# Adding each expert's output on chip to rows that are read back, instead of letting the DMA add them in DRAM

## The chip, the cores and the metric

The kernel runs on one core of one Trainium2 chip. The metric is the device time of one execution in microseconds (us); a kernel's time is the median of its runs. The engines of the core are TensorE (PE; its weight loads are listed as PEld), VectorE (DVE), ScalarE (ACT), GpSimd (POOL) and SyncE (SP). All of them run their own instruction streams in order and meet through semaphores. Data moves between DRAM and the on-chip memory through 16 DMA engines, which are fed by queues: here one hardware queue (q1) that SP fills, and one software queue (q0) that GpSimd fills.

## The reference

One decoder layer with 512 tokens of width 2048, in fp32: a mixer (sparse attention beside a convolution), cross-attention into 256 memory rows, and a mixture of experts (MoE). The change lies almost wholly in the last part. A token picks the best of 4 groups, and in that group the best two of 8 experts; each expert is a SwiGLU of hidden width 512, and the two outputs are added with their weights:

```python
grp = argmax(xf @ rg_w + rg_b)                    # 1 of 4 groups
top_v, top_i = lax.top_k(le_g, 2)                 # 2 of the group's 8 experts
w_tok = w_grp[:, None] * softmax(top_v)
h = silu(xb @ w_gate[e]) * (xb @ w_up[e])         # the rows of expert e
y = (h @ w_down[e]) * wb[:, None]
out = zeros(...).at[tok_buf].add(y)
x = layer_norm(DEEPNORM_ALPHA * x + out, ln3_g, ln3_b)
```

So each token's row before the last normalisation is the sum of its own row `x2` and of two experts' rows (the kernel divides the weights by alpha instead of scaling `x2`, which the normalisation allows). The order of the two additions doesn't matter beyond rounding.

## The kernel before

Everything up to the MoE is one long PE-bound stretch of 1500 us, in which weights pass through a ring of tiles (`wr`, split on ACT and DVE into two fp32r parts, `wh` and `wl`, L78). In it `bias_setup` (L250ff) makes the table of relative positions: `vec`, written to `vec_d`, and 16 copies to `toe_d`, all issued by SP between loads of `w_in`.

At the end of cross-attention four tiles of 128 tokens are normalised (`rs` on POOL at L150, the scaling on DVE at L161) and transposed for the router (`x2T`, L72). With gain and bias applied (L829, L830, on DVE and POOL), each tile of 1 MB is written twice by SP: to `x2_d` (L831; `x_d` in the profile), from which experts read their rows, and to `acc_d` (L833), onto which the outputs are added. The router then finds for each token its two experts and its place in their lists.

`build` (L1017) turns these into lists, one for each expert, of up to two blocks of 64 tokens. Per expert it makes 8 one-hot matrices `oh` of 128x128 on DVE (L1024) and 8 matmuls (L1025), each with a one-hot matrix as stationary operand and the 4 columns of `rhs` (token number twice, and the weight in two parts) as moving operand. `lists` (L1034) makes from it row numbers `ix` and weights `wl`. Each half of a token row (1024 floats, 4 KB) has its own number; a place that is not filled gets a number out of bounds, for which the transfer does nothing. Two experts are built before the loop, two at its start, and then four at a time, every fourth turn.

The loop over 32 experts (L1142) streams 12 tiles of 1 MB of weights an expert (4 gate, 4 up, 4 down). SP issues each load (`load_next`, L1107) as soon as one of 19 slots `mr` is released, with a row of loads in flight. In turn e, PE does gate and up of expert e (L1275) in four quarters, then transposes the rows of expert e+1 (`prep`, L1263), then the down product of expert e-1 (L1303) and the transposes of the hidden rows (L1291). Work of a second block, which only 4 experts have, stands in `If` blocks of its own (L1152, L1168, L1172, L1175, L1183), which all engines enter or skip on a count. The down product lands in PSUM (`dn`); `scaled` (L1305ff) multiplies it by the weight, one half on ACT and one on DVE (L1309), into `y`; `put_rows` (L1204) writes `y` to the rows of `acc_d` with an indirect DMA that adds to what is there. `gather` (L1209) reads the rows of expert e+2 with an indirect DMA (L1201) into `xe`, of which there are two for each block. Both are issued by POOL on the software queue.

What sets the order: the code is written in program order, a list scheduler orders each engine's stream by priorities, and the engines run it in that order. After the last expert SP reads `acc_d` back and the last normalisation follows.

## Time and profile before

| | us |
|---|---|
| median of 3 runs (2614.37 to 2618.21) | 2615.86 |
| the profiled execution | 2621.89 |
| its span in the profile | 2619.9 |
| PE busy in the span | 2393.8 |
| DVE busy | 1136.1 |
| ACT busy | 727.6 |
| POOL busy | 193.1 |
| start of the first expert's gate and up products | 1551.4 |
| last output of an expert scaled | 2576.8 |

The page divides the span into 40 slices; PE is busy for 90% or more in nearly all of them, and the 16 DMA engines are above 90% only from the MoE on. The table is thus no answer to what bounds the kernel: each stage is read for itself. The profile's times below are microseconds from the start of the span.

### The profile page before, as it was taken

The page shows a single profiled execution, that of the slowest core. Times are in us where ns is not written, and L with a number is a line of the kernel's source. Part 1 is how long each engine was busy: PE and PEld are TensorE (multiplying, and loading weights), DVE is VectorE, ACT ScalarE, POOL GpSimd, SP SyncE. Part 2 cuts the span into 40 slices and gives each one's busy share as a digit, 9 for nine tenths or more (in the row PEclk, how much of TensorE's full clock was granted, in tenths as well). Part 3 has the DMA queues.
Part 4 walks back from the last instruction along what each step waited for, and adds up shares of the span by engine and source line. Part 5 has one row for each costly group of instructions (what it writes and reads, how often), then busy time and mean ns, then how long its engine had stood idle before and what let it go on. Part 6 is the DMA issues. An engine that isn't in the chain of part 4 may idle for free. (4 is left out here: it accounts for less than half of the span.)

```text
span 2619.9 us, 31427 instructions
## 1 busy us (share of the span) xinstructions
PE 2393.8 (91%) x11298; PEld 1566.2 (60%) x11299; DVE 1136.1 (43%) x2406; ACT 727.6 (28%) x1286; POOL 193.1 (7%) x247
## 2 busy tenths in 40 slices
PE   6999899999999999999999968999998889999973
PEld 5788676789878778788888843333333344333320
DVE  5848985488877643543453542111110101101004
ACT  4323125467766522333321310101000001010103
POOL 1100000000000000000000220101000100110101
PEclk9999999989999999999999968999999999999996
DMA  4235324433334533332542397999999999999995
GB/s 139 87 109 172 111 75 118 125 101 121 105 112 132 202 126 105 128 106 96 196 146 97 126 377 303 418 416 412 409 407 408 413 399 416 347 400 415 416 415 220
DMA packets 195539, 617.30 MB, mean 236 GB/s; under 512 B 43241, under 2 KB 92577, under 8 KB 142096
## 3 DMA queue, kind: packets, MB, share of 16 engines
q1 hardware_dynamic: 178048, 568.08, 57.0%
q0 software_dynamic: 17296, 46.66, 5.8%
q8 instruction: 117, 1.92, 0.3%
q14 instruction: 78, 0.64, 0.1%
HBM read 593.64 MB, written 47.23 MB: 245 GB/s over the span
## 5 line engine op out<-in xcount | busy, mean ns | idle before, releaser
L1275 PE MATMUL gu<-mr,xeT 128*64 128x512 f32 x2048 | 539.7, 613 | 56.4 <-DMA mr<-moe_w_up 23.6
L78 DVE TENSOR_TENSOR wl<-wr,wh 128x1024 fp32r<-128x1024 f32 (+1 forms) x248 | 294.5, 1190 | 374.7 <-ACT wh L78 374.0
L78 ACT ACTIVATE wh<-wr 128x1024 fp32r<-128x1024 f32 (+2 forms) x250 | 256.0, 1026 | 618.2 <-PE pd L83 287.6
L1275 PEld LDWEIGHTS gu<-mr,xeT 128*64 128x64 f32 x2048 | 172.1, 139 | 357.5 <-issue 276.9
L1303 PE MATMUL dn<-mr,hT 128*64 128x512 f32 x1152 | 295.4, 603 | 15.3 <-PEq L1183 12.9
L1284 DVE TENSOR_TENSOR h<-gu,sg 64x256 f32<-64x256 f32 x72 | 30.7, 427 | 446.7 <-ACT sg L1283 446.3
L82 PE MATMUL pd<-xT,wh 128*128 128x512 f32 x512 | 203.8, 405 | 15.5 <-DVE v L550 5.3
L83 PE MATMUL pd<-xT,wh 128*128 128x512 f32 x512 | 205.1, 401 | 0.0
L1303 PEld LDWEIGHTS dn<-mr,hT 128*64 128x64 f32 x1152 | 92.3, 138 | 171.6 <-issue 150.5
L84 PE MATMUL pd<-xT,wl 128*128 128x512 f32 x512 | 183.2, 399 | 1.6 <-DVE wl L78 1.6
L1283 ACT ACTIVATE sg<-gu 64x256 f32<-64x256 f32 x72 | 27.0, 375 | 543.2 <-PE gu L1275 526.3
L445 DVE SCALAR_TENSOR_TENSOR acc<-u,wc,acc 128x512 f32<-128x512 f32 x240 | 164.9, 750 | 0.3
L82 PEld LDWEIGHTS pd<-xT,wh 128*128 128x128 f32 x512 | 99.1, 194 | 41.1 <-issue 14.6
L1309 DVE TENSOR_SCALAR y<-dn,wlm 128x512 f32<-128x512 f32 x36 | 27.0, 751 | 220.1 <-PE dn L1303 210.9
L84 PEld LDWEIGHTS pd<-xT,wl 128*128 128x128 f32 x512 | 98.0, 191 | 24.5 <-DVE wl L78 2.3
L83 PEld LDWEIGHTS pd<-xT,wh 128*128 128x128 f32 x512 | 98.7, 193 | 20.7 <-issue 1.2
L1205 POOL DMA_INDIRECT acc_d<-y,ixm x36 | 57.0, 1583 | 729.2 <-ACT xeT L68 257.8
L83 PE MATMUL pd<-x1T,wh 128*128 128x512 f32 x256 | 101.9, 399 | 0.0
L83 PE MATMUL pd<-wl,oT 128*128 128x512 f32 x256 | 100.1, 391 | 1.1 <-DVE wl L78 1.1
L84 PE MATMUL pd<-x1T,wl 128*128 128x512 f32 x256 | 100.5, 398 | 0.0
L84 PE MATMUL pd<-wh,oT 128*128 128x512 f32 x256 | 99.3, 390 | 0.0
L82 PE MATMUL pd<-x1T,wh 128*128 128x512 f32 x256 | 98.5, 400 | 0.8 <-ACT x1T L175 0.8
(410 smaller groups left out, 3940.7 us busy)
## 6 DMA issues: line engine op xcount, KB each, us to landing
mr<-moe_w_down SPq DMA_DIRECT2D x128, 1024.0 KB, 15.7
mr<-moe_w_gate SPq DMA_DIRECT2D x127, 1024.0 KB, 15.9
mr<-moe_w_up SPq DMA_DIRECT2D x127, 1024.0 KB, 16.0
wr<-xa_wkv SPq DMA_DIRECT2D x64, 512.0 KB, 3.7
wr<-w_in SPq DMA_DIRECT2D x112, 256.0 KB, 3.0
wr<-w_out SPq DMA_DIRECT2D x32, 512.0 KB, 3.5
wr<-xa_wq SPq DMA_DIRECT2D x32, 512.0 KB, 3.5
wr<-xa_wo SPq DMA_DIRECT2D x32, 512.0 KB, 3.5
```

The lines of the kernel that those rows point to most:

```text
L78: return self.nc.scalar.activation(h, src, AF.Copy), eng.tensor_tensor(l, src, h.bitcast(F32), op=ALU.subtract)
L82: mm(out, lhsT=ah, rhs=bh, start=start, stop=False)
L83: mm(out, lhsT=ah, rhs=bl, start=False, stop=False)
L84: mm(out, lhsT=al, rhs=bh, start=False, stop=stop)
L445: nc.vector.scalar_tensor_tensor(a, u[:, k:k + S], wc[:, j, k:k + 1], a, op0=ALU.mult, op1=ALU.add)
L1205: self.nc.gpsimd.indirect_dma_start(out=self.acc_d.rearrange("s (h d) -> (s h) d", h=2), out_offset=bass.IndirectOffsetOnAxis(ap=ix, axis= ...
L1275: self.nc.tensor.matmul(bank[64 * a:64 * a + 64], lhsT=xT[:, 4 * q + c, :], rhs=w[a][:, c * 512:(c + 1) * 512], start=(q == c == 0), stop= ...
L1283: nc.scalar.activation(sg[64:128, sl], bank[0:64, sl], AF.Silu)
L1284: nc.vector.tensor_tensor(h[64 * b:64 * b + 64], bank[64:128, sl], sg[64:128, sl], op=ALU.mult)
L1303: self.nc.tensor.matmul(out[j][64 * a:64 * a + 64], lhsT=hT[:, r, :], rhs=w[:, 1024 * a + 512 * j:1024 * a + 512 * j + 512], start=(r == 0 ...
L1309: self.nc.vector.tensor_scalar(y[:, 512:], out[1], wl, None, op0=ALU.mult)
```

## The change

The sum is made on chip. A token's row has two experts; `x2` stays in `xe` after the first one's product, and the output is added to it there. For the second expert, what the first wrote is read back from `acc_d` over `xe`, and the output is added to that.

- `x2` is written to `x2_d` alone. `acc_d` is instead filled with zeros much earlier, in `bias_setup`: a tile of 256 zeros a partition, and four writes of 1 MB in pieces of 1 KB, on SP.
- `xe` has four tiles for the first block and three for the second, seven in place of four; all are cleared on POOL at the start of the MoE.
- `put_rows` and `scaled` become `add_rows`: two DVE operations that read `dn` from PSUM and `xe`, and write `xe`; then an indirect write of `xe`, without the add in the DMA.
- `get_rows(self.acc_d, ...)` reads the rows back, through the list `got`, which holds only tokens whose second expert (in order of number) this is. The column `fo` of `rhs`, made by three operations on POOL, says which it is.
- `build` compares two token tiles at once (two comparisons an expert, 128x256) with one `oh` buffer, takes the 4 columns as stationary operand and the one-hot matrix as moving operand (4 matmuls), and turns the result with two small transposes an expert. It is called for two experts every second turn.
- Two more `If` blocks stand in a turn: the read-back of a second block, and the gather of a second block (which moves from `gather` to after the put).
- If an expert has more than 128 tokens, `acc_d` is first set to `x2` and every row is read back.

```diff
@@ bias_setup
             nc.sync.dma_start(self.vec_d, vec)
+            z = bs.tile([P, 256], F32, name="zero")
+            nc.gpsimd.memset(z, 0.0)
+            for i in range(4):
+                nc.sync.dma_start(self.acc_d[i * P:(i + 1) * P, :].rearrange("p (c d) -> p c d", d=256), z[:, None, :].to_broadcast([P, 8, 256]))
@@ end of cross-attention
-                    nc.sync.dma_start(self.x2_d[i * P:(i + 1) * P, :], x)
-                    self.x2w[i] = nc.sync.dma_start(self.acc_d[i * P:(i + 1) * P, :], x)
+                    self.x2w[i] = nc.sync.dma_start(self.x2_d[i * P:(i + 1) * P, :], x)
@@ router
+        gp = nc.gpsimd.tensor_tensor
+        tt(r1, r1, r2, op=ALU.is_gt)
+        gp(fo, o1, o2, op=ALU.subtract)
+        gp(fo, fo, bc(r1, 32), op=ALU.mult)
+        gp(rhs[:, :, :, 1], fo, o2, op=ALU.add)
-        nc.vector.tensor_copy(rhs[:, :, :, 1], bc(self.tok, 32))
@@ build
         for j in range(n):
-            for b in range(2):
-                for i in range(4):
-                    oh = pool.tile([P, P], F32R, tag="oh", bufs=4, name="oh")
-                    nc.vector.tensor_scalar(oh, self.ios[:, b, :], self.pos[:, i, e0 + j:e0 + j + 1], None, op0=ALU.is_equal)
-                    nc.tensor.matmul(spv[:, 2 * j + b, :], lhsT=oh, rhs=self.rhs[:, i, e0 + j, :], start=(i == 0), stop=(i == 3))
+            for i in range(4):
+                if i % 2 == 0:
+                    oh = pool.tile([P, 2, P], F32R, tag="oh", bufs=1, name="oh")
+                    nc.vector.tensor_tensor(oh, self.ios[:, None, :].to_broadcast([P, 2, P]), self.pos[:, i:i + 2, e0 + j:e0 + j + 1].to_broadcast([P, 2, P]), op=ALU.is_equal)
+                nc.tensor.matmul(sp[:4, j * P:(j + 1) * P], lhsT=self.rhs[:, i, e0 + j, :], rhs=oh[:, i % 2, :], start=(i == 0), stop=(i == 3))
+        for j in range(n):
+            ls = pool.tile([4, 2, 2, 64], F32, tag="ls", bufs=1, name="ls")
+            nc.vector.tensor_copy(ls, sp[:4, j * P:(j + 1) * P].rearrange("p (b o t) -> p b o t", b=2, o=1).to_broadcast([4, 2, 2, 64]))
+            for b in range(2):
+                nc.tensor.transpose(sp[:, m:m + 4], ls[:, b].rearrange("p o t -> p (o t)"), self.ident[:4, :4])
@@ the MoE's tiles
-        self.xe = [[self.mx.tile([P, D // 2], F32, name=f"xe{j}{b}") for b in range(2)] for j in range(2)]
+        self.xes = [[self.mx.tile([P, D // 2], F32, name=f"xe{j}{b}") for j in range(4 - b)] for b in range(2)]
@@ the loop
-                    if (e + 3) % 4 == 0 and e + 3 < NE:
-                        build(e + 3, 4)
+                    if (e + 3) % 2 == 0 and e + 3 < NE:
+                        build(e + 3, 2)
...
-                    self.put_rows(self.scaled(y, self.where[e - 1, 0][1]), self.where[e - 1, 0][0])
+                    self.add_rows(self.xe(e - 1, 0), y, *self.where[e - 1, 0][1::-1])
...
+                if 0 < e < NE:
+                    self.get_rows(self.acc_d, self.xe(e, 0), self.where[e, 0][2])
+                    with tc.If(self.many(e, [T.Pool]) > 64):
+                        self.get_rows(self.acc_d, self.xe(e, 1), self.where[e, 1][2])
+                if e + 2 < NE:
+                    self.gather(e + 2, 1)
@@ the put
+    def add_rows(self, t, out, wl, ix):
+        for a in range(2):
+            x = t[:, 512 * a:512 * a + 512]
+            self.nc.vector.scalar_tensor_tensor(x, out[a], wl, x, op0=ALU.mult, op1=ALU.add)
         self.nc.gpsimd.indirect_dma_start(out=..., in_=t, in_offset=None,
-                                          bounds_check=2 * S - 1, oob_is_err=False, compute_op=ALU.add)
+                                          bounds_check=2 * S - 1, oob_is_err=False)
```

The change also moves instructions. On SP, in `bias_setup`, the loads of `w_in` and the table's writes stood so before the change (`wr` are the ring's weight tiles):

```order
L92 DMA wr_1887<-w_in 128x2x256 x2
L92 DMA wr_1918<-w_in 128x2x256 x2
L92 DMA wr_1949<-w_in 128x2x256 x2
L92 DMA wr_2056<-w_in 128x2x256 x2
L92 DMA wr_2087<-w_in 128x2x256 x2
L268 DMA vec_d_2377<-vec_2387 16x640
```

and on the same queue SP now has:

```order
L92 DMA wr_1887<-w_in 128x2x256 x2
L273 DMA acc_d_83<-zero_2422 1024x1x256
L92 DMA wr_1918<-w_in 128x2x256 x2
L273 DMA acc_d_83<-zero_2422 1024x1x256 x3
L92 DMA wr_1949<-w_in 128x2x256 x2
L92 DMA wr_2056<-w_in 128x2x256 x2
L92 DMA wr_2087<-w_in 128x2x256 x2
L268 DMA vec_d_2377<-vec_2387 16x640
```

One of the four zero writes now stands ahead of the load of tile 1918, and the other three ahead of that of tile 1949.

On DVE, where the last token tile goes through its normalisation (`rs` and L161) to the router's copy `x2T`, with gain and bias (L829, L830) of the tile between, the rows stood so before:

```order
L151 SCALAR_TENSOR_TENSOR rs_12381<-mv_12379,rs_12381 128x1
L161 TENSOR_SCALAR xr1_11116<-xr1_11116,rs_12381 128x512 x2
L829 TENSOR_TENSOR xr1_11116<-xr1_11116,gb2_12125 128x512 x2
L830 TENSOR_TENSOR xr1_11116<-xr1_11116,gb2_12125 128x512
L829 TENSOR_TENSOR xr1_11116<-xr1_11116,gb2_12125 128x512
L830 TENSOR_TENSOR xr1_11116<-xr1_11116,gb2_12125 128x512
L72 COPY x2T_12124<-ptr_12389 128x512
```

and now (lines are 5 further down, L824 having become L829):

```order
L834 TENSOR_TENSOR xr1_11122<-xr1_11122,gb2_12131 128x512 x2
L835 TENSOR_TENSOR xr1_11122<-xr1_11122,gb2_12131 128x512
L834 TENSOR_TENSOR xr1_11122<-xr1_11122,gb2_12131 128x512
L151 SCALAR_TENSOR_TENSOR rs_12384<-mv_12382,rs_12384 128x1
L835 TENSOR_TENSOR xr1_11122<-xr1_11122,gb2_12131 128x512
L161 TENSOR_SCALAR xr1_11122<-xr1_11122,rs_12384 128x512 x2
L829 TENSOR_TENSOR L_11693<-lgp_11127,rbias_11691 128x36
L72 COPY x2T_12130<-ptr_12392 128x512
```

Gain and bias that stood between the normalisation and the copy are now ahead of the normalisation.

On PE, in the turn in which the lists of later experts are made (`oh` one-hot matrices, `tp` their PSUM, `xe` the next expert's rows), before:

```order
L1025 MATMUL tp<-rhs,oh 128x4 x4
L1303 MATMUL dn<-mr,hT 64x512 x5
L1263 MATMUL tp<-ident,xe_12468 128x128 x4
L1025 MATMUL tp<-rhs,oh 128x4 x4
L1275 MATMUL gu<-mr,xeT 64x512 x8
L1025 MATMUL tp<-rhs,oh 128x4 x4
L1263 MATMUL tp<-ident,xe_12468 128x128 x4
L1025 MATMUL tp<-rhs,oh 128x4 x5
```

and now:

```order
L1037 MATMUL tp<-oh,rhs 4x128 x2
L1348 MATMUL dn<-mr,hT 64x512 x3
L1308 MATMUL tp<-ident,xe_12472 128x128 x4
L1037 MATMUL tp<-oh,rhs 4x128 x2
L1320 MATMUL gu<-mr,xeT 64x512 x8
L1037 MATMUL tp<-oh,rhs 4x128 x2
L1308 MATMUL tp<-ident,xe_12472 128x128 x4
L1043 MATMUL tp<-ident,ls 128x4 x2
```

Where sets of four matmuls with one-hot matrices stood, sets of two stand, followed by the small transposes (L1043), in every second turn instead of every fourth.

## Rows read from the trace of the kernel before

**Rows 1.** Four stretches: us, busy PE, PEld, DVE, ACT, POOL, granted clock, DMA share, GB/s.
```profile
1549.00:1628.00 79.00, 71.39 (x300) 28.45 (x300) 16.30 (x68) 6.63 (x15) 3.71 (x3) 0.89 0.79 319
1628.00:2125.00 497.00, 449.85 (x1927) 171.81 (x1928) 72.12 (x236) 44.64 (x104) 48.80 (x38) 0.98 1.01 409
2125.00:2283.00 158.00, 156.35 (x709) 67.52 (x707) 23.76 (x71) 17.42 (x41) 13.11 (x10) 0.99 0.98 388
2283.00:2567.00 284.00, 255.45 (x1086) 92.36 (x1086) 29.40 (x79) 24.34 (x56) 23.64 (x17) 0.98 1.01 408
```

**Rows 2.** Waits of PE, 1628 to 2125 us: waited for, total us, times, longest.
```profile
PE gu L1275 <- DMA mr<-moe_w_up: 17.9, 13, 3.1
PE gu L1275 <- PEq L1172: 9.5, 10, 1.3
PE gu L1275 <- PEq L1152: 2.5, 13, 0.6
```

**Rows 3.** Software DMA queue, 1628 to 2125, then 2283 to 2567 (packets, MB, share).
```profile
q0 software_dynamic: 5472, 8.83, 6.5%
...
q0 software_dynamic: 2727, 4.03, 6.4%
```

**Rows 4.** Same queue: a put (2365.5–2375.5), gathers (2088.5–2098.5), empty gather (2127–2137), plain write (420–432).
```profile
q0 software_dynamic: 144, 0.45, 22.7%
...
q0 software_dynamic: 256, 0.57, 14.6%
...
q0 software_dynamic: 144, 0.03, 1.4%
...
q0 software_dynamic: 638, 2.09, 47.6%
```

**Rows 5.** The loop's start: PE's matmul groups and longest wait, 1549–1628; one window.
```profile
L1025 PE MATMUL tp<-rhs,oh 128*128 128x4 f32 x48 | 8.2, 265 | 5.1 <-PEq L1152 4.8 <-DVE oh L1024 0.2
...
PE tp L1263 <- DMA xe<-x_d,ixm: 11.0, 1, 11.0
...
1580.00:1590.00 10.00, 9.70 (x44) 2.97 (x40) 0.00 (x0) 0.38 (x1) 1.04 (x2) 1.00 0.31 125
```

**Rows 6.** Timelines of POOL (two rows) and DVE at the end of cross-attention.
```profile
1499.35 3.84 POOL L1074 MEMSET xe<- 128x1024 f32 x4
...
1505.66 0.56 POOL L150 TENSOR_TENSOR rs<-mv,mhalf 128x1 f32<-128x1 f32 x1
...
1507.50 2.86 DVE L161 TENSOR_SCALAR xr<-xr,rs 128x512 f32<-128x512 f32 x2
...
1515.57 0.68 DVE L72 COPY x2T<-ptr 128x512 f32<-128x512 f32 x1
```

**Rows 7.** Timelines of SP, ACT, PE in `bias_setup`; the page's row of landings.
```profile
223.64 19.85 SPq L92 DMA_DIRECT2D wr<-w_in  x10
...
256.58 1.06 ACT L78 ACTIVATE wh<-wr 128x1024 fp32r<-128x1024 f32 x1
...
272.93 2.07 PE L457 MATMUL cmu<-acc,one 128*128 128x512 f32 x2 [7.91 <-DVE acc L445]
...
wr<-w_in SPq DMA_DIRECT2D x112, 256.0 KB, 3.0
```

**Rows 8.** PE's groups in the one list building of the crowded stretch, 2222 to 2248.
```profile
L1025 PE MATMUL tp<-rhs,oh 128*128 128x4 f32 x32 | 5.7, 262 | 0.1
```

**Rows 9.** Two consecutive puts on POOL; landings of gathers and puts (last number, us).
```profile
1867.42 1.58 POOL L1205 DMA_INDIRECT acc_d<-y,ixm  x1 [16.29 <-ACT xeT L68]
...
1893.78 1.58 POOL L1205 DMA_INDIRECT acc_d<-y,ixm  x1 [23.41 <-ACT xeT L68]
...
xe<-x_d,ixm POOLq DMA_INDIRECT x36, 10.1
acc_d<-y,ixm POOLq DMA_INDIRECT x36, 9.1
```

**Rows 10.** The page's group of DVE's half of `scaled`: busy us, mean ns.
```profile
L1309 DVE TENSOR_SCALAR y<-dn,wlm 128x512 f32<-128x512 f32 x36 | 27.0, 751 | 220.1 <-PE dn L1303 210.9
```

More of the change, by code (lines that the diff above doesn't have):

```diff
@@ L1134, in moe @@
                     self.load_next(nc.gpsimd if n < 2 else None)
-            build = lambda e, n: self.build(self.mx, self.tp.tile([P, 512], F32, name="tp"), e, n)
+            with tc.If(self.many(32, [T.Pool]) > P):
+                nc.gpsimd.dma_start(self.acc_d, self.x2_d)
+            build = lambda e, n: self.build(self.mx, self.tp.tile([P, 512], F32, name="tp"), e, n)()
             W = lambda e: lambda r: self.raws[e, r]
@@ L1278, in gated @@
         nc = self.nc
-        sg = self.my.tile([P, 512], F32, name="sg", tag="sg", bufs=1)
         h = self.my.tile([P, 256], F32, name="h", tag="h", bufs=1)
```

100 lines of the change are left out of this document (55 added, 45 removed).

## The prediction

> **What bounds the kernel now.** I read the busy times by stage first, then PE's waits in each stage, then the DMA queues in the same stretches, and last the timelines at the two places that the change touches outside the loop. Up to the MoE the kernel is held by PE and, for short whiles, by DVE; the change touches only two places there. In the loop the bound changes four times [rows 1]. From 1549 to 1628 us the DMA engines are only 79% busy: the weight slots are full and PE is late. In one ten-microsecond window the share falls to 0.31 while PE is busy for 9.70 us [rows 5]. From 1628 to 2125 the share is 1.01 and the rate 409 GB/s: the DMA engines are the bound, and PE waits for weights, 17.9 us on the gate and up tiles of one kind alone [rows 2]. From 2125 to 2283, where experts with a second block follow one another, PE is busy for 156 of 158 us: PE is the bound. From 2283 to 2567 it is the DMA again, with 1.01. So a microsecond of PE work is worth something in the first and third stretch, and a microsecond of DMA time in the second and fourth. All sums below are against the profiled execution (2621.89 us, 6.03 above the median of 2615.86); the change in time is then taken off the median.
>
> **DMA price of a row.** One row is 4 KB (0.0041 MB). A put alone in 10 us moved 0.45 MB, 110 rows, in 22.7% of 16 engines, so 36.3 engine-us [rows 4]. A gather in which nearly every place was empty took 1.4% of the same, 2.24 engine-us, for 144 packets of which 7 were rows: about 8 ns an empty place. Two gathers moved 0.57 MB, 139 rows, in 14.6%, 23.4 engine-us; without 117 empty places 22.4, so 161 ns a row. The put, less its 34 empty places, comes to 327 ns a row: twice a gather. A plain write out of SBUF in 4 KB packets is shown once, in the convolution's part: 2.09 MB, 510 packets, in 47.6% of 16 engines over 12 us, 91.4 engine-us, or 177 ns with the small packets taken off. So each output row now costs 327, and afterwards a plain write of 161 to 177 plus a read-back for every second row, half of 161. That saves 69 to 85 ns a row; I take 77.
>
> How many rows? Share and megabytes of the software queue give two equations [rows 3]. From 1628 to 2125: 6.5% of 16 x 497 us is 517 engine-us, 26 of them for 3316 empty places; 8.83 MB are 2156 rows. With 161 ns for all of them, 143 us are left over, which at the extra 166 ns of a put are 860 puts. From 2283 to 2567 the same gives 291 engine-us, 14 off, 984 rows, and 710 puts. The saving is 860 x 77 / 16 = 4.1 us and 710 x 77 / 16 = 3.4 us. Each read-back also carries some 100 empty places: 17 puts of the first stretch and 11 of the last by 100 x 8 / 16 ns is 0.9 and 0.6 us. What remains is **-3.2 us** (-1.7 to -4.0) and **-2.8 us** (-1.5 to -3.5). PE's waits on loads leave room for the first.
>
> **Does the read-back fit?** The turn of expert e needs what expert e-1 wrote. After a put (1.58 us on POOL) come its landing (9.1), the issue of the read-back (taken as another 1.58) and its landing (10.1): 22.4 us. Puts of two consecutive turns stand 26.4 us apart [rows 9], so the read-back is there some 4 us before DVE needs it, and `dn` has two buffers that let PE go on if it is not. Behind POOL's wait for the landing stands the gather of the rows three turns ahead, which the four `xe` tiles allow for: nothing. DVE gets one more operation of 0.75 us [rows 10] in place of ACT's half, on engines that idle: nothing.
>
> **The loop's start**, PE-bound. Before the third expert's weights are asked for, PE spends 8.2 us on 48 list matmuls (32 for four experts, 16 for two), 265 ns each, and waits another 4.8 us of which one `If` chain makes the most [rows 5]. Afterwards four experts are built in this stretch instead of six, each with 4 matmuls and 2 transposes instead of 8 matmuls. At 265 ns each that is 24 x 0.265 = 6.4 us, 1.8 saved; no row shows a 4-column stationary and a 128-column moving operand, and between half that price and one and a half it is 3.2 to 9.5 us, from 5 saved to 1.3 lost. The sets are smaller and wait on one `oh` buffer, but PE has other matmuls between. Two turns carry two more skipped `If`s, which I price below at about 1 us a turn. On the other side fewer sets and fewer list waits lie ahead of the first products. I take **-2.5** (-5 to +1); it is the least certain term. That 4 MB of `acc_d` are no longer written before the loop buys nothing: the DMA engines idle later in this stretch anyway, for want of slots.
>
> **The crowded stretch**, 2125 to 2283, PE-bound. One building of four experts costs PE 5.7 us [rows 8]; afterwards two buildings of two experts, by the same count 24 operations, some 4 to 5.7: -1.7 to 0. The gain of the DMA is lost here, since PE does not wait for it. Against it stand the two new `If`s a turn. A skipped `If` between matmuls costs PE 0.19 us (2.5 us in 13 waits), but one that stands in a clump with other control work 0.95 (9.5 in 10) [rows 2], and the change puts the new ones in a clump. So some four turns cost 4 x 0.2 to 4 x 1 us, 0.8 to 4. Between these ends I take the lower half, since the new `If`s are branches alone for PE, and the sum is **0** (-2 to +4).
> [...]
>
> **The end of cross-attention.** Seven tiles are cleared on POOL instead of four, at 3.84 / 4 = 0.96 us, so `rs` of the last token tile, which runs at 1505.66 close behind the clearing, comes 2.9 us later [rows 6]. The way from it to the lists and the first gather is the path: PE waits 11.0 us for the first expert's rows [rows 5]. But DVE now does the tile's gain and bias ahead of the normalisation and not between it and the copy `x2T`. Today the normalisation ends at 1510.36 and the copy starts at 1515.57, so up to 5.2 us stand between; the transposes on PE need some of that. I take 3.4 back: **-0.5** (-2.5 to +3.3, with the list's three POOL operations).
>
> **The zero fill.** Four megabytes at 409 GB/s [rows 1] are 10.3 us, at the plain write's price 11.4. Five pairs of `w_in` loads are issued from 223.64 to 243.5, and the fifth pair is split on ACT at 256.58, 13.1 us after its issue; a load lands in 3.0 [rows 7]. The fill stands ahead of the last three of them, so their lead falls from 10.1 us to about zero. DVE is the one that suffers: PE waits 7.91 us for it at 272.93, so what delays the splits delays the path. **+1.5** (0 to +4).
>
> **The tail.** The second DVE operation runs behind the first, +0.75; the last put, with few rows, lands earlier by up to a microsecond. **+0.2** (-0.5 to +1).
>
> **Sum.** +1.5 - 0.5 - 2.5 - 3.2 + 0 - 2.8 + 0.2 = -7.3 us: 2614.6 in the profiled execution, 2608.6 in the median.
>
> **Rivals.**
> *The add was not the price.* Suppose the 327 ns belong to writing scattered rows and stay. Then nothing is saved and the read-back is added: (860 + 710) x 81 / 16 = 7.9 us, and 1.5 for the empty places. The sum becomes -1.3 + 9.4 = +8.1, a median of 2624, slower. It decides at a scattered write of 327 - 81 - 15 = 231 ns (15 being the empty places, 1.5 us x 16 / 1570). For it: no row shows a scattered plain write. Against it: the plain write of 177 ns and the exact factor of two between put and gather. Chance 0.08.
> *Branches and the fill eat it.* The `If`s cost 1 us each turn in both PE-bound stretches (crowded +3.5, start 0), the rest as forecast: -1.3, a median of 2614.6, no change. With the fill at +4 instead, and all else as forecast, -4.8. For it: PE's waits of 0.95 us behind control work. Against it: list work falls at the same places. Chance 0.28.
> *The read-back is late*, so the row isn't in `xe` when DVE wants it: the round trip of 22 us becomes the loop's period where landings of 11 to 12 us meet waits on POOL. It decides at 26.4 us; each microsecond above costs one in each of some 20 turns, thus +20 and a median of about 2630. Against it: 4 us of slack and longer turns where blocks are large. Chance 0.04.
> The forecast, with what is better than it, has 0.60.
>
> **How the numbers follow.** A measurement of this kernel tells 0.2%, about 5.2 us, from no change. Faster than that has 0.60, within it 0.28, slower 0.12. All terms at their better ends give -17.5, 2598; the worse end of the no-change case and the nearer part of the slower ones reach 2620. This leaves out about 2 in 10, most of it slower.
>
> **What would show it.** The software queue should carry more megabytes in the two DMA-bound stretches, and take fewer engine-microseconds for them; a put should show about 160 to 180 ns a row. The stretch from the third expert's load request to the end of loads should shorten by about 6 us in total. PE should reach the first gate product within 3 us of 1551 plus the fill's delay, and its wait at 273 should grow by 0 to 4 us. DVE waiting for a read-back, in any turn, would speak for the third rival; a put at over 231 ns a row for the first; PE waits behind the new `If`s of about a microsecond in the crowded stretch for the second. The forecast is wrong above all if the saved DMA time does not shorten the two DMA-bound stretches, or if the order of the list work in the start leaves PE waiting where it now has matmuls.

## The result, and the profile after

The change made the kernel 0.7% slower, where the forecast was 7 us faster and its range ended at 2620 us.

| | median of the runs | profiled execution's span |
|---|---|---|
| before | 2616.3 us (2614.37 to 2618.21) | 2619.9 us |
| after | 2636.86 us (2635.68 to 2639.86) | 2635.4 us |

The ratio is 1.0072, 95% interval 1.006 to 1.0084. The spans differ by 15.5 us and the medians by 20.6, because before's profiled execution lies 5.6 us above its median and after's 0.3. The stages below are read from the spans and carry 15.5; a stage reading is good to about 2 us (a kernel with the same start as before differed from it by 1.9 at the loop's start).

After's stretches, in the columns of [rows 1]:

```profile
1549.00:1628.00 79.00, 65.45 (x280) 23.47 (x281) 13.12 (x39) 6.24 (x14) 5.17 (x5) 0.91 0.89 364
1628.00:2125.00 497.00, 443.54 (x1928) 157.40 (x1926) 82.18 (x209) 33.38 (x88) 51.45 (x51) 0.98 1.01 417
2125.00:2283.00 158.00, 144.94 (x660) 53.64 (x656) 23.85 (x60) 11.77 (x31) 15.05 (x15) 0.99 0.89 361
2283.00:2567.00 284.00, 255.74 (x1076) 88.69 (x1077) 42.72 (x99) 18.28 (x48) 29.72 (x30) 0.94 1.00 412
```

The third row has changed its nature (a stretch of fixed times, so not quite the same work). Before, PE was busy for 156.35 of these 158 us; now for 144.94, and the DMA share fell from 0.98 to 0.89 as well. Neither engine is the bound there any more: both wait.

To see where the time went, I count the 384 weight loads in both traces and compare when the same load is issued. Before issues load 42 at 1630.0, load 228 at 2132.2, load 294 at 2319.7 and the last (383) at 2559.9, so these cut the loop into the stages of the prediction. In the table stands this kernel's stage minus before's, in us. "PE order" says whether the second block's down products stand ahead of the first block's last four ("early", as in before) or behind all of them ("late").

| kernel | PE order | up to 42 | 42–228 (DMA) | 228–294 (crowded) | 294–383 (DMA) | to the end | sum |
|---|---|---|---|---|---|---|---|
| after | late | -2.5 | -6.8 | **+13.5** | +0.2 | **+11.2** | +15.5 |
| noget | early | +0.3 | -14.3 | 0.0 | -10.0 | +1.4 | -22.6 |
| getfree | early | -1.8 | -4.6 | +3.2 | -6.9 | +2.5 | -7.6 |
| plainput | early | -1.9 | -12.1 | +1.7 | -8.6 | +0.1 | -20.8 |
| newbuild | early | -8.0 | +0.6 | 0.0 | -0.5 | +2.1 | -5.9 |
| noget_old | early | +5.5 | -11.2 | -1.8 | -6.1 | +0.1 | -13.4 |
| oldbuild | late | +3.1 | -5.9 | +13.9 | +2.7 | +10.2 | +24.0 |
| getaside | late | -3.1 | -5.8 | +20.2 | +0.9 | +3.0 | +15.2 |
| getF | late | -0.7 | -7.8 | +13.0 | +2.4 | +6.6 | +13.4 |
| getFx | late | -3.6 | -7.7 | +17.8 | -2.2 | +5.9 | +10.2 |
| x2first | late | -2.3 | -7.0 | +19.6 | -3.6 | +3.7 | +10.4 |
| addfirst | late | -3.4 | -6.9 | +13.5 | +1.9 | +6.2 | +11.3 |
| noifs | late | -0.1 | -6.2 | +19.1 | +4.2 | +3.3 | +20.2 |

The kernels other than after are the experiments below; hfirst, mix and getFxa have their stages there in words. Two stages hold after's loss: the crowded one and the end.

**The DMA's price came out as forecast.** The software queue after, from 1628 to 2125 and from 2283 to 2567 (answers to [rows 3]):

```profile
q0 software_dynamic: 7073, 8.84, 4.9%
...
q0 software_dynamic: 4178, 5.52, 5.3%
```

In the first, 4.9% of 16 x 497 us are 390 engine-us; 8.84 MB are 2158 rows, the other 4915 packets are empty places at 8 ns (39 us), so a row, whether gathered, put or read back, costs 350 / 2158 = 162 ns. The second gives 218 / 1348 = 162 too. A put alone (1734.7 to 1744) moved 0.51 MB, 124 rows, in 13.5%: 161 ns a row without its 20 empty places. A plain scattered put costs what a gather does; the 327 ns belonged to the addition.

**The crowded stage.** SP's timeline where the stage breaks, of after (start, us, the instruction):

```profile
2210.87 0.33 SPq L1137 DMA_DIRECT2D mr<-moe_w_up  x1
2213.34 0.33 SPq L1137 DMA_DIRECT2D mr<-moe_w_gate  x1
2226.88 0.33 SPq L1137 DMA_DIRECT2D mr<-moe_w_up  x1
2227.26 0.42 SPq L1137 DMA_DIRECT2D mr<-moe_w_gate  x1
2227.73 0.42 SPq L1137 DMA_DIRECT2D mr<-moe_w_up  x1
2236.35 0.33 SPq L1137 DMA_DIRECT2D mr<-moe_w_gate  x1
2236.72 0.43 SPq L1137 DMA_DIRECT2D mr<-moe_w_up  x1
```

No weight is asked for during 13.5 us, then three within one, then none for 8.6. In the same stretch (2195 to 2260) before asks for one about every 2.5 us and pauses once for longer, 9.1 us. What PE does in that gap, and just behind it:

```profile
2218.09 3.60 PE L1320 MATMUL gu<-mr,xeT 128*64 128x512 f32 x16
2221.52 7.04 PE L1348 MATMUL dn<-mr,hT 128*64 128x512 f32 x32
2228.49 1.23 PE L1308 MATMUL tp<-ident,xe 128*128 128x128 f32 x8
2230.26 0.41 PE L1336 MATMUL tp<-ident,h 128*128 128x128 f32 x2 [0.54 <-ACT xT L68]
2230.60 1.07 PE L1320 MATMUL gu<-mr,xeT 128*64 128x512 f32 x2
2232.22 0.41 PE L1336 MATMUL tp<-ident,h 128*128 128x128 f32 x2 [0.55 <-DVE h L1329]
```

(The profile has two records for each product of 512 columns.) The eight `gu` products are the first quarter of the *next* expert; only then come the second block's down products (second row), which free four slots, and behind them the second block's transposes and both transposes of `h` stand bare, each waiting half a microsecond for ACT or DVE. PE's waits of the whole stage (2119.6 to 2333.1) are many small ones; the largest four (waited for, total, times, longest) are one of this kind, two of the list building and one for weights:

```profile
PE tp L1336 <- DVE h L1329: 3.6, 3, 1.5
PE tp L1037 <- DVE oh L1036: 2.1, 4, 0.5
PE gu L1320 <- DMA mr<-moe_w_up: 1.5, 1, 1.5
PE tp L1043 <- DVE ls L1040: 1.5, 3, 0.5
```

All waits at the transposes of `h` (L1336) together are 5.8 us there; in getfree, the experiment below without the read-back's wait, they are 0.8, and the two of the list building are 3.1 for the 3.6 here. Before's stage has 0.6 at the transposes of `h`. `h` has one buffer, so the second block's `h` can't be made before the first one's transposes have read it; before has down products between the two, after at most a `gu` product.

**The end.** The chain of waits of after, its last part (start, us, what):

```profile
2566.57 8.40 DMA acc_d<-xe,ixm
...
2575.74 4.09 DMA xe<-acc_d,got
...
2581.62 15.71 DMA acc_d<-xe,ixm
2597.48 0.34 SPq L1366
```

and two rows of the timelines of DVE and PE there:

```profile
2579.93 1.41 DVE L1249 SCALAR_TENSOR_TENSOR xe<-dn,wlm,xe 128x512 f32<-128x512 f32 x2 [13.64 <-DMA xe<-acc_d,got]
...
2580.78 10.01 PE L1348 MATMUL dn<-mr,hT 128*64 128x512 f32 x32 [6.27 <-DVE xe L1249]
```

Put, landing, read-back, addition and put follow one another in single file; the last DMA piece ends when the puts of the last two experts have landed. The down products of the last expert even wait 6.27 us for DVE to empty `dn`, which DVE can't before the read-back lands. Before read its sums from 2582.69; after does from 2597.48.

**The start.** PE's wait at the zero fill is [rows 7]'s 7.91 us grown to 8.67; the fill is all but free. But the first gather leaves 4.7 us later (1540.45 before):

```profile
273.12 2.07 PE L462 MATMUL cmu<-acc,one 128*128 128x512 f32 x2 [8.67 <-DVE acc L450]
...
1545.17 1.18 POOL L1242 DMA_INDIRECT xe<-x_d,ixm  x1 [12.28 <-DMA mr<-moe_w_up]
```

### The profile page after: what moved, and what is told of

Its sections match the earlier page's. It is cut to its first block, busy times and chain, and to the rows that moved or that the text cites. A ratio compares the mean times of both kernels' runs of the same rounds, so it can differ in the third digit from the quotient of the medians.

```text
span 2635.4 us, 31338 instructions
## 1 busy us (share of the span) xinstructions
PE 2376.9 (90%) x11234; PEld 1529.1 (58%) x11235; DVE 1158.5 (44%) x2350; ACT 703.5 (27%) x1250; POOL 211.8 (8%) x289
## 5 line engine op out<-in xcount | busy, mean ns | idle before, releaser
L1320 PE MATMUL gu<-mr,xeT 128*64 128x512 f32 x2048 | 545.7, 620 | 30.6 <-PEq L1187 15.9
L1348 PE MATMUL dn<-mr,hT 128*64 128x512 f32 x1152 | 261.7, 606 | 7.7 <-DVE xe L1249 6.3
L82 PE MATMUL pd<-xT,wh 128*128 128x512 f32 x512 | 203.2, 404 | 15.2 <-DVE v L555 5.3
L1348 PEld LDWEIGHTS dn<-mr,hT 128*64 128x64 f32 x1152 | 81.9, 139 | 162.8 <-issue 143.9
L1036 DVE TENSOR_TENSOR oh<-ios,pos 128x256 fp32r<-128x256 f32 x64 | 26.8, 420 | 223.0 <-PE tp L1037 222.5
L1249 DVE SCALAR_TENSOR_TENSOR xe<-dn,wlm,xe 128x512 f32<-128x512 f32 x72 | 51.0, 746 | 157.3 <-DMA xe<-acc_d,got 89.7
L84 PEld LDWEIGHTS pd<-xT,wl 128*128 128x128 f32 x512 | 97.8, 191 | 24.5 <-DVE wl L78 2.3
L83 PEld LDWEIGHTS pd<-xT,wh 128*128 128x128 f32 x512 | 98.2, 192 | 20.6 <-issue 1.2
```

Of the source, the lines that this page charges most:

```text
L82: mm(out, lhsT=ah, rhs=bh, start=start, stop=False)
L83: mm(out, lhsT=ah, rhs=bl, start=False, stop=False)
L84: mm(out, lhsT=al, rhs=bh, start=False, stop=stop)
L1036: nc.vector.tensor_tensor(oh, self.ios[:, None, :].to_broadcast([P, 2, P]), self.pos[:, i:i + 2, e0 + j:e0 + j + 1].to_broadcast([P, 2, P] ...
L1249: self.nc.vector.scalar_tensor_tensor(x, out[a], wl, x, op0=ALU.mult, op1=ALU.add)
L1320: self.nc.tensor.matmul(bank[64 * a:64 * a + 64], lhsT=xT[:, 4 * q + c, :], rhs=w[a][:, c * 512:(c + 1) * 512], start=(q == c == 0), stop= ...
```

## The experiments

Each edit is against the kernel after unless it says before. Ratios are to the kernel before, with 95% intervals.

### What the parts are worth

**plainput.** The kernel before without the addition in the DMA:

```
-  bounds_check=2 * S - 1, oob_is_err=False, compute_op=ALU.add)
+  bounds_check=2 * S - 1, oob_is_err=False)
```

> The kernel before, with the put of the outputs as a plain indirect write: the add in the DMA is left out, so rows hold one expert's output and not the sum. Theory: the add costs half the put's DMA time (327 ns a row against 161 to 177), so 1570 rows in the two DMA-bound stretches give back 14 to 16 us less what the PE-bound stretch between doesn't pass on: 2601 to 2606. Rival: the 327 ns belong to scattered writes: 2616 as before.

2599.36 us, 0.9928 [0.9911, 0.9944], 1.6 us below the expected range. The addition costs 19 us, all of it in the two DMA-bound stages (-12.1 and -8.6).

**noget.** The kernel after without its read-backs:

```
-  self.get_rows(self.acc_d, self.xe(e, 0), self.where[e, 0][2])
-  with tc.If(self.many(e, [T.Pool]) > 64):
-      self.get_rows(self.acc_d, self.xe(e, 1), self.where[e, 1][2])
```

> The changed kernel without the read-backs: neither the rows written by a first expert are read back, nor is there an If for them; a token's row thus misses its first expert's output. Theory: the read-backs cost their DMA time (1024 rows x 161 ns / 16 = 10 us, some 8 of it in the DMA-bound stretches, and 1 to 2 for empty places), the round trip write, landing, read-back, addition of the last three experts (11 us at the end) and POOL's wait for the landing in front of the gathers (1 to 4 us in the crowded stretch): 2612 to 2617 in all, and the last put starts within 2 us of the last down product. Rival: the order of PE's work and the list building cost the time: then only the DMA time comes back, 2626 to 2629.

2598.06 us, 0.9919 [0.9902, 0.9935], 14 us below what was expected. So the read-backs cost 38.8 us (2636.9 less 2598.1), twice what the addition had cost. The gain was real and is lost to what replaces it.

**oldbuild**, **noget_old.** The list building of before put back into after and into noget:

```
-  nc.tensor.matmul(sp[:4, j * P:(j + 1) * P], lhsT=self.rhs[:, i, e0 + j, :], rhs=oh[:, i % 2, :], ...)
+  nc.tensor.matmul(spv[:, 2 * j + b, :], lhsT=oh, rhs=self.rhs[:, i, e0 + j, :], ...)
...
-      build(e + 3, 2)
+      build(e + 3, 4)
```

> The changed kernel with the list building of before: 8 one-hot matrices of 128x128 an expert in 4 buffers, as stationary operand, 4 moving columns, four experts at a time. Theory: the new building is cheaper on PE (0.28 us for two matmuls against 0.6 for four) but waits on its single one-hot buffer and on the copy ahead of its transposes, 16 us of PE waits in the loop, of which those in the PE-bound start and crowded stretches count, 2 us ahead of the first gather and 4 in the crowded stretch; the old one gives that back and takes its 8 and 6 us of matmuls: 2635 to 2640, no clear difference. Rival: the new building is what makes the crowded stretch 14.7 us longer: 2622 to 2627.

> The changed kernel without the read-backs and with the list building of before, so that what is left of the change is the sum in xe with four and three tiles, the plain put, the zero fill and the moved gathers (first experts' outputs are missing in rows). Theory: it stands within 4 us of the kernel without the read-backs, and 10 to 15 us above the kernel before with a plain put (2599), which has the same transfers but two skipped blocks instead of three on POOL ahead of the first gather (2 us) and PE's old order in the crowded stretch. Rival: the read-backs are all that makes the difference: 2600 to 2604.

2643.31 us, 1.0091 [1.0074, 1.0108]; and 2605.71 us, 0.9946 [0.993, 0.9963]. Both were expected otherwise: oldbuild as fast as after, noget_old within 4 us of noget. The new building is worth 6.4 and 7.6 us, 5.6 and 5.2 of them by load 42. The group that answers to [rows 5] says why, in after from 1549 to 1628:

```profile
L1037 PE MATMUL tp<-oh,rhs 128*4 128x128 f32 x16 | 2.4, 233 | 5.3 <-PEq L1187 4.7 <-DVE oh L1036 0.6
L1043 PE MATMUL tp<-ident,ls 4*128 4x4 f32 x8 | 1.1, 209 | 0.0
```

3.5 us of list work, where 48 matmuls took 8.2.

**newbuild.** The kernel before, with only the new list building (the same lines the other way round, and the two transposes an expert).

> Edit: the kernel before (rows added by the DMA, no read-backs, its buffers), with only the list building of the kernel after: the one-hot matrix as moving operand, two comparisons an expert, two experts at a time. Nothing of the computation is left out. Theory 2 (the new building is worth the same 6.5 to 7.6 us as in the two kernels in which the old one was put back): 2608.5 to 2612. Rival (in the kernel before, the adding puts make the DMA engines the bound from 1628 us on, and they swallow what the start gains): 2614 to 2619, no change.

2616.52 us, 0.9991 [0.9982, 1.0], against 2619.06 for before beside it, as the rival had it. The 8.0 us at load 42 are mostly kept to the end in the trace (-5.9), but the median shows 2.5; before's trace is the one that lies 5.6 us above its median. It is the only kernel that computes everything and isn't slower than before, and it can't be told from no change.

### What the read-backs' 39 us consist of

**getfree.** The read-back takes x2's rows in place of the sums, so it has nothing to wait for:

```
-  self.get_rows(self.acc_d, self.xe(e, 0), self.where[e, 0][2])
+  self.get_rows(self.x2_d, self.xe(e, 0), self.where[e, 0][2])
...
```

(the second block's read-back likewise.)

> Edit: the kernel after, with each read-back taken from x2 (the rows that the gathers read) in place of the sums in DRAM. Lists, sizes, count and place of the transfers, the third skipped block on POOL and the dependence of the addition on the read-back all stay; only the read no longer waits for the landing of the put of the expert before, and the order on PE that the scheduler works out from that wait changes with it (down products of an expert and the next transposes of h again ahead of the next expert's gate and up products, as in the kernel before). It leaves out: the rows added are x2's, not the sums so far, so the output lacks parts of the sums. Theory 1 (of the 38.8 us that the read-backs cost, most is POOL's wait for the put's landing, with the gathers behind it, and what the scheduler makes of it): near the kernel without read-backs, 2600 to 2610. Rival (the transfers themselves, 4.2 MB with some 1,700 empty places, and the third skipped block): 2628 to 2637. Between: 2610 to 2628 splits the price.

2611.94 us, 0.9978 [0.9967, 0.9989], just above theory 1's range, where the price is split. The transfers with their skipped block cost 13.9 us (against noget), their waiting 25 us. By the spans (after less getfree, 23 us) the waiting is 10 in the crowded stage, 7 in the last one and 9 at the end, less 3 in the two first columns. With the wait the order on PE changes as well, since the scheduler that sets each engine's order reckons with it. PE's rows around the down products of one turn, of after and of getfree, branches left out:

```
after                                    getfree
gu<-mr,xeT 64x512 x7                     gu<-mr,xeT 64x512 x7
tp<-ident,xe 128x128 x8                  dn<-mr,hT 64x512 x4
dn<-mr,hT 64x512 x16                     tp<-ident,h 128x128 x2
gu<-mr,xeT 64x512 x8   (next expert)     dn<-mr,hT 64x512 x8
dn<-mr,hT 64x512 x16   (second block)    dn<-mr,hT 64x512 x16  (second block)
tp<-ident,xe 128x128 x8                  tp<-ident,h 128x128 x2
tp<-ident,h 128x128 x2                   dn<-mr,hT 64x512 x4
```

**getaside.** The read-back's rows go into the tile that is free next, which no addition reads: the wait of POOL and the transfers stay, DVE's wait goes.

```
-  self.get_rows(self.acc_d, self.xe(e, 0), self.where[e, 0][2])
+  self.get_rows(self.acc_d, self.xe(e + 3, 0), self.where[e, 0][2])
...
```

(the second block's likewise, into its next tile, `e + 2`.)

> The changed kernel, in which the rows read back land in a tile that expert e does not use (that of the expert three turns on, whose gather overwrites it), so that nobody waits for them; a row thus misses its first expert's output. The same transfers, waits of POOL for the put's landing and If blocks as the changed kernel. Without read-backs the time fell from 2637 to 2598. Theory: of these 39 us the transfers themselves make 8 to 12, the rest is the dependence of the addition on the read-back, through DVE's and PE's order and the single pair of down-product banks in PSUM: 2606 to 2612. Rival: POOL's wait for the landing, with gathers of later experts behind it, and the read-backs' DMA time make it: 2625 to 2637.

2636.94 us, 1.0066 [1.0049, 1.0082]: the same as after, as the rival had it. But it is no clean test of DVE's wait. The tile that takes the rows is the next one to be gathered into, so that gather now waits for the read-back, and PE for the gather, which it did once in after (13.1 us, ahead of the loop's first product). PE's waits of getaside, 1550 to 2590:

```profile
PE tp L1308 <- DMA xe<-x_d,ixm: 25.0, 4, 12.7
...
PE tp L1308 <- DMA xe<-acc_d,got: 4.3, 1, 4.3
```

In the crowded stage PE's waits for such rows (and 2.9 us of issue) make 11.3 us, for 1.1 in after. By an estimate the stage's +20.2 would without them be about +10, so DVE's wait is worth some 3 to 4 us of after's +13.5 there. The end gains 8 us (+3.0 for +11.2); x2first below gains nearly as much with DVE's wait in place, so that isn't shown to be its price either.

**getF.** The read-back is issued a turn later, so that on POOL the next gathers stand ahead of its wait:

```
+  if e > 1:
+      self.get_rows(self.acc_d, self.xe(e - 1, 0), self.where[e - 1, 0][2])
+      self.get_rows(self.acc_d, self.xe(e - 1, 1), self.where[e - 1, 1][2])
   y = self.down(W(e - 1), hT)
```

(the block behind the additions goes.)

> Edit: the kernel after, with an expert's read-back issued a turn of the expert loop later, just ahead of the addition that needs it, and with no skipped block around the second one. On POOL the gathers of the next expert then stand ahead of the read-back's wait for the put's landing, where in the kernel after they stand behind it; the order on PE around the down products stays that of the kernel after (first quarter of the next expert's gate and up products ahead of the second block's down products). Nothing of the computation is left out; experts with one block add 128 empty places each. Theory A (the 25 us that went with the read-back's wait came from POOL, with the gathers queued behind it at run time): 2612 to 2622. Theory B (they came from the order on PE that the scheduler set by that wait): 2630 to 2640.

2634.14 us, 1.0053 [1.0036, 1.0069]. The crowded stage keeps its +13.0 and the gap in the loads is still there; SP's timeline of getF:

```profile
2214.15 0.33 SPq L1137 DMA_DIRECT2D mr<-moe_w_gate  x1
2230.01 0.33 SPq L1137 DMA_DIRECT2D mr<-moe_w_up  x1
```

and the stage in one row each (between loads 228 and 294) of before, after, getF and getfree, columns as in [rows 1]:

```profile
2132.20:2319.70 187.50, 184.09 (x828) 77.15 (x826) 25.26 (x73) 19.17 (x44) 16.31 (x12) 0.99 0.98 385
...
2122.90:2323.80 200.90, 184.66 (x833) 67.16 (x830) 29.92 (x72) 13.68 (x36) 21.60 (x22) 0.98 0.90 366
...
2123.70:2324.20 200.50, 184.51 (x826) 66.27 (x824) 28.71 (x69) 13.68 (x36) 22.89 (x23) 0.98 0.92 366
...
2125.80:2316.50 190.70, 183.19 (x832) 64.62 (x830) 33.49 (x83) 13.72 (x36) 21.39 (x22) 0.98 0.98 395
```

PE's work is the same 183 to 185 us in all four; what differs is its idle time: 3.4, 16.2, 16.0 and 7.5 us. So the queue on POOL alone isn't the cause, and DVE's wait alone isn't either, by the estimate under getaside. What divides all the kernels of the table without exception is the order on PE: +13 to +20 us with the late order, -1.8 to +3.2 with the early one. A second mark goes with it: in every early kernel a pair of `h`'s transposes stands among the down products, in every late one they stand behind all of them, and so they do in getFxa, mix and hfirst below (+17.6, +24.5 and +42.5).

**hfirst.** An attempt at the early order: the next expert's first quarter is held behind the transposes of `h`.

```
-  self.gate_up(W(e), xT, b0, (q,))
+  with tc.issue_after(self.turned.ins) if e and q == 0 else ExitStack():
+      self.gate_up(W(e), xT, b0, (q,))
...
```

> Edit: the kernel after, with the first quarter of an expert's gate and up products held on PE until the transposes of the last expert's h have been issued; that puts the order on PE back near that of the kernel before, and leaves every transfer, wait of POOL and list as they are. Nothing of the computation is left out. Theory 1a (the 13 us of the crowded stretch come from the order on PE that the scheduler chose, which releases the slots of the second block late): 2620 to 2627. Theory 1b (they come from POOL's wait at run time, with the gathers behind it, whatever PE's order): 2633 to 2640.

2679.69 us, 1.0223 [1.0208, 1.0239], outside both theories' ranges. The order it got was a third one: all down products first, and nothing behind which ACT and DVE could make `h`. PE's waits of hfirst, 1550 to 2600:

```profile
PE dn L1350 <- issue: 35.1, 17, 3.0
PE tp L1338 <- PEq L1208: 25.1, 24, 1.3
...
PE dn L1350 <- ACT sg L1330: 14.8, 10, 1.8
```

It shows how much PE's order is worth here (42 us in the crowded stage), and leaves 1a untested: no kernel had both the read-back's wait and the early order. That the order alone costs the 10 us, without the wait that brings it, was therefore not shown directly.

**noifs.** The `If`s around the second block's gathers and read-backs removed, so POOL has two blocks fewer each turn.

```
-  with tc.If(self.many(e, [T.Pool]) > 64):
-      self.get_rows(self.acc_d, self.xe(e, 1), self.where[e, 1][2])
+  self.get_rows(self.acc_d, self.xe(e, 1), self.where[e, 1][2])
...
-  with self.tc.If(self.many(e, [mybir.EngineType.Pool]) > 64) if b else ExitStack():
+  if True:
```

> The changed kernel without the two new If blocks: read-back and gather of a second block are issued for every expert; for most of them every place is out of bounds. Theory: in the crowded stretch (2120 to 2333 us) PE idles 16.6 us where it idled 4.6, and a third to a half of the 12 us more come from the clump of branches in which nothing else is scheduled; without two of them the stretch is 3 to 6 us shorter, the additional 60 transfers of empty places cost 1 to 2 us of DMA time: about 2633. Rival: PE idles because its matmuls are in another order (the down product and the next expert's first quarter ahead of the transposes, one one-hot buffer), and branches alone cost little: 2636 to 2639.

2642.62 us, 1.0102 [1.0085, 1.0119]: slower, outside both ranges. At 8 ns a place, 60 transfers of 128 places more are an estimated 3.8 us of the 16 engines; PE's order changed too, so the rest is not divided. As a test of branches on PE it is void: the two `If`s load their count for POOL alone (`[T.Pool]`), and in the trace's record POOL alone branches at their lines, in after too. At the start the blocks do cost, on POOL; without the two of the gathers the first one leaves 3.4 us earlier:

```profile
1541.79 1.18 POOL L1241 DMA_INDIRECT xe<-x_d,ixm  x1 [11.22 <-DMA mr<-moe_w_up]
```

**x2first**, **getFx.** All seven loads that wait for an x2 write go behind the fourth, in after and in getF.

```
-  QUEUE = (2, 1, 1, 3)
+  QUEUE = (0, 0, 0, 7)
```

> The changed kernel with one number changed: none of the seven weight tiles that are loaded ahead of the loop stands before the fourth write of x2 on SP's queue. Theory: the first gather waits for that write, which lies behind 4 MB of weights in the DMA queue; with it ahead, the gather leaves some 3 to 4 us earlier (list ready at 1541.4 us, gather at 1545.2), PE's first gate product is at 1551.5 to 1552.5 instead of 1555.6, and the time falls by 3 to 4 us to about 2633. Rival: the gather is late because of the slower list chain on one one-hot buffer (ready 2 us later than before) and of POOL's queue; then it leaves at 1545 all the same and the time stays at 2637.

> Edit: getF, and all seven loads that wait for an x2 write are put behind the fourth one, as in x2first. The order on PE changes too: of the next expert's gate and up products only one of the first eight stands ahead of the second block's down products. Theory A: 4 to 6 us below getF, as x2first lay below the kernel after. Theory B: 10 us or more below getF, since the slots of the second block come free earlier.

2631.0 us, 1.0049 [1.0033, 1.0066]; and 2631.73 us, 1.0041 [1.0027, 1.0055], 2.4 us below getF, short of both theories. In x2first the gather still leaves at 1544.83, so the x2 write wasn't what it waited for, and the 5.9 us that it gains on after have another source. Both bring an order in which one product instead of eight stands ahead of the second block's: the crowded stage gets worse (+19.6, +17.8), so those eight products are not the harm in the late order; in getaside, at +20.2, none of them stands there. (The mean granted clock is lower in x2first and getFx, 0.93 of full speed in the crowded stage in the one and 0.94 in the other (2120 to 2333), for after's 0.98, and PE's work in x2first 187.0 us for 184.7, which is some of it.) What these kernels gain comes in the two last stages. At the end it goes with where the third-last expert's addition stands on DVE: in after behind the last gating,

```profile
2564.42 0.43 DVE L1329 TENSOR_TENSOR h<-gu,sg 64x256 f32<-64x256 f32 x1 [0.44 <-ACT sg L1328]
2564.88 1.41 DVE L1249 SCALAR_TENSOR_TENSOR xe<-dn,wlm,xe 128x512 f32<-128x512 f32 x2
```

in x2first at 2542.10, 26 us ahead of it. It stands ahead of it in all late kernels of the table whose end is at +6.2 or less, and behind it in the three above that (after, oldbuild, getF). The gain in the last DMA-bound stage is not settled.

**addfirst**, **getFxa.** DVE's gating is held behind the addition of two experts before, so that the last puts leave early; in after and in getFx.

```
-  h = self.gated(b0)
+  with tc.issue_after(self.added0.ins) if e > 1 else ExitStack():
+      h = self.gated(b0)
...
```

> The changed kernel, in which the SwiGLU products of expert e are queued behind the addition of expert e-2 on DVE. Theory: at the end the addition of expert 29 stands behind the products of expert 31 (2564.9 us, though its down product was done at 2543), so that write, read-back, addition and write of 29, 30 and 31 follow one another after the last load; in the new order expert 29 is added near 2545 and the last put starts 8 to 11 us earlier: about 2627. Rival: the end is late because the last loads are late (4.3 us after those of before) and because of the round trip of the last two experts alone, which stays: a gain under 3 us, or a loss where DVE now waits for read-backs in front of the products.

> Edit: getFx, with the gating of an expert on DVE held behind the addition of the expert two before it, as in addfirst, so that the puts of the last experts leave earlier. If the end of the program is still bound by the puts of the last three experts: 3 to 5 us below getFx, and by either theory the lowest of the kernels that compute everything (2603 to 2615). If the read-back that is issued late already sets that addition: no change or up to 10 us above getFx, since the gating then waits behind a landing.

2632.17 us, 1.0055 [1.0038, 1.0072]; and 2628.22 us, 1.0032 [1.0021, 1.0044]. In after the end falls from +11.2 to +6.2: nearly half of it was an addition that stood on DVE behind the last gating. That is 4.7 us in the median, about half of what was expected. getFxa lies 3.5 us below getFx; it is the best kernel with read-backs, and still slower than before and far above the 2603 to 2615 that were expected.

**mix.** A token's first expert writes x2 plus its output plainly (masked rows), its second adds in the DMA, so that nothing is read back; two puts a turn, and adding puts alone for second blocks and the last three experts.

```
-  self.add_rows(self.xe(e - 1, 0), y, *self.where[e - 1, 0][1::-1])
+  self.put_sum(e - 1, 0, y)     # DVE: wl * y + masked x2 rows
...
+  put(first)
+  put(second, compute_op=ALU.add)
```

> A version without read-back and with half the adds in the DMA: rows of a token's first expert are written plainly as x2 + output, those of the second, with x2 masked out on ACT, with an adding put; acc_d starts as x2 again (no zero fill), the last three experts and second blocks use adding puts alone. New list building. Theory: half of the adds' 19 us (the gain of plain puts) come back, with 1 to 2 us for the empty places of two puts a turn and 7 us for the cheaper building: 2602 to 2610, faster than both. Rival: two puts a turn, each waiting for the other's landing on POOL, 18 us of a turn's 26, delay the gathers behind them, and the scheduler puts PE's work in another order again: above 2616.

2650.07 us, 1.0119 [1.0103, 1.0136], as the rival had it. The first DMA-bound stage gains nothing (+0.3) and the crowded one loses 24.5, with the late order here too. It is no way round the read-back.

## Why the prediction was wrong

Its steps, by the spans:

| term | forecast | measured |
|---|---|---|
| zero fill | +1.5 | +0.4 |
| end of cross-attention, up to the first gate product | -0.5 | +3.8 |
| the loop's start, to load 42 | -2.5 | -6.7 |
| first DMA-bound stage | -3.2 | -6.8 |
| crowded stretch | 0 | **+13.5** |
| last DMA-bound stage | -2.8 | +0.2 |
| tail | +0.2 | **+11.2** |

(The first gate product starts at 1551.42 before and 1555.58 after: +4.2, of which 0.4 is the fill's.)

- **The step that failed is "Does the read-back fit? ... nothing".** It weighed a round trip of 22.4 us against a turn of 26.4 us and asked only whether the rows would be there when DVE wants them. getfree shows what the wait costs instead of nothing: 25 of the read-backs' 39 us, the other 14 being the transfers. Two things were left out. The read-back's wait also moves PE's instructions: the compiled order of after has the transposes of `h` behind all down products, and no term had that: PE's cost was priced by counting its instructions, not by where they stand. In the crowded stage the kernel loses 13.5 us, 10.3 more than getfree; 5.0 of these are waits at those transposes. That the order makes the loss fits all the kernels, but no run isolates it. And the last experts have no later turn to hide the round trip in: put, read-back, addition, put is the end of the program (+11.2 for +0.2). With the wait gone, getfree lands at 2611.94, within 3.4 us of the forecast.
- **"`dn` has two buffers that let PE go on" was wrong.** The two halves of one expert's output take both. The 6.27 us for which the last down products wait for DVE are that.
- **The price of the put was right; the waits moved the transfers.** 162 ns was measured for the assumed 161 to 177. The software queue between loads 42 and 228, then between loads 294 and 383, of before, getfree and after:

```profile
q0 software_dynamic: 5598, 8.86, 6.4%
...
q0 software_dynamic: 7896, 10.28, 5.7%
...
q0 software_dynamic: 7101, 8.91, 5.0%
...
q0 software_dynamic: 2205, 2.98, 5.4%
...
q0 software_dynamic: 3312, 3.63, 4.4%
...
q0 software_dynamic: 3456, 4.40, 5.0%
```

  In getfree, whose read-backs wait for no put, the shares come to 3.8 and 2.7 us less than before, for the forecast 3.2 and 2.8. After reads back as many rows, but POOL issues its transfers later: the first stage has 1.4 MB less than getfree's, the last 0.8 MB more. So the queue gives 7.4 us back in the first and 1.0 in the last, where the time changed by -6.8 and +0.2. The two terms together, -6.0, came to -6.6. Of the 7 us by which after's last stage is longer than getfree's, the later transfers explain some 2; the rest is open.
- **The end of cross-attention.** Clearing three more tiles was hidden: the copy `x2T` comes 0.8 us later, 0.4 of it the fill's, much as forecast. What came instead was POOL's control work: three skipped blocks with a DMA inside stand ahead of the first gather where before has two, and the list is ready 2 us later (1541.25 for 1539.29).
- **The loop's start** was right in kind and mis-sized, -2.5 for -6.7: the list work takes 3.5 us, near the better bound of 3.2 and 4.7 less than before. Where the other 2 us come from is not shown.
- **The price of the two new `If`s for PE** (0.8 to 4 us in the crowded stretch) was a term for nothing: PE has no branch at their lines in after's trace, where POOL alone has 35 and 36 (L1215, L1254). Its waits behind control work in that stage are 3.4 us, 3.8 before.
- **The rivals.** "The add was not the price" is refuted by plainput and the 162 ns. "Branches and the fill eat it" had the fill at 0.4, and its branches are not on PE. "The read-back is late" named the right resource with 0.04, but put its price on the wrong thing: the loop didn't take the round trip as its period. DVE does stand waiting for read-backs, 89.7 us in seven waits; what that costs inside the loop is only estimated (getaside, 3 to 4 us of the crowded stage).

## What to carry to other kernels

A read-back that depends on one's own last write was not paid by the transfer alone here (14 of 39 us): ask what stands behind the wait in each engine's compiled order, whether the wait has changed that order, and compare that order before and after around the busiest stretch, even on engines that the change doesn't name. Price the end of a loop apart from its turns: a round trip that a turn hides has nothing to hide it after the last one (+11.2 us here). And a transfer that waits can slip out of one stage into another with a different bound (here 1.4 MB less than getfree's in the first DMA-bound stage, 0.8 MB more in the last): compare the megabytes by stage before the times.

## What the runs showed of the hardware

- A scattered put of a 4 KB row cost 161 ns of one DMA engine (after, a put alone), as much as a gather ([rows 4], 161 ns); the same put with addition 327 ns ([rows 4]). In the kernel the addition of 2048 such rows made 19 us (plainput).
- On POOL a skipped `If` with an indirect DMA inside was not a branch alone in these traces. Their record of control instructions, which the views leave out, has ahead of the first gather two such blocks in before and three in after, each with a semaphore instruction of 1.64 to 1.67 us; with the load of the count a block takes 2.2 to 2.4 us (the first one, which waits for the count, longer). With one block (noifs) that gather leaves 3.4 us earlier than with three.
